# A hybrid encoder layer: the 16 meta keys of attention taken once per head, as rows of one score bank, with one float32r product per group in place of a float32 one

## The chip, the cores and the metric

The kernel runs on one core of one Trainium2 chip. The metric is device time in microseconds (us); of several runs the median counts. A core has a matrix engine (PE; its weight loads are shown apart as PEld), a vector engine (DVE), a scalar engine (ACT), a general engine (POOL), and a queue engine that issues transfers (SP). PE writes into PSUM, which has 8 banks of 128 rows by 512 float32 values; DVE and ACT read and write it.

## The reference

One encoder layer on a sequence of 1024 tokens with 16 learned "meta" tokens ahead of it, 1040 positions in all, model width 1024. All values are float32.

```python
hn = rms_norm(h, ln1_g)
p = hn @ w_in                    # c_q | c_kv | k_rope | x_rnn | x_gate
o_attn = mla_group(...)          # 8 heads; q and k of 96 per head, v of 64
o_rnn = rglru_group(...)         # gated linear recurrence, both directions
h = h + concat(rms_norm(o_attn), rms_norm(o_rnn)) @ w_out
hn = rms_norm(h, ln2_g)
h = h + (silu(hn @ w_gate) * (hn @ w_up)) @ w_down
return h[:, 16:]
```

Within `mla_group`, q and k are normalised per head and rotated, and each query attends to all 1040 keys:

```python
s = einsum('bhqd,bhkd->bhqk', q, k) * 96 ** -0.5
o = einsum('bhqk,bhkd->bhqd', softmax(s), v)
```

The outputs of the meta queries aren't returned and nothing after the attention mixes positions, so the kernel computes attention for the 1024 real queries alone. The meta keys and values are needed.

## The kernel before

**Precision.** PE has a fast product with rounded operands (float32r, F32R in the code) and a slower float32 one. To reach float32 the kernel splits each operand into a rounded part (hi) and the remainder (lo), and adds three float32r products: hi by hi, hi by lo, lo by hi (`mm3`, `hi_lo`, lines 61 to 73). ACT writes hi, DVE subtracts it from the source to give lo.

**Stages by time.** The input projections and the recurrence come first, up to some 197 us. Then come the attention's own projections (`kv_half`, `q_half`, lines 514 to 566), normalisation (`kv_norm`, `q_norm`), and the first head's preparation. The attention loop runs from 257 to 518 us. The output projection and the feed-forward follow up to the end. Most of the program is ordered by a planner; the attention loop (lines 911 to 1000 and on) is under a manual schedule: each engine executes in the order in which the code is written.

**Key blocks.** A head's keys are 8 blocks of 128 real keys (kb 0 to 7) and one block of the 16 meta keys (kb 8), which stand behind the real ones in the tiles `kh`, `kl` (hi and lo of the transposed keys, 96 rows, 1040 columns). The values are in `vhl`: for each real block and head 64 columns of lo, 64 of hi and two columns of ones. The meta values are in `vf` in plain float32: 64 columns and two of ones (line 470, written at line 526).

**The loop.** A group is one head and one half (512) of the queries, so there are 16 groups (`g`, even for the first half, odd for the second) of 9 items each, one item for each key block. One step of the loop handles one item and issues, in this order:

- whatever the step before left in `late` (evacuations, transposes of the next head's q and k, small sums);
- `score`: three products of 512 columns into a bank T (lines 706 to 708), with the keys as weights, and ACT's exponential in place (line 714). A row of ones in the keys and a row with the negated maximum in the queries subtract the maximum. For the meta block the bank has 16 rows only, and the exponential goes to an SBUF tile `e` (lines 709 to 712);
- `max_chunk`: products of the next group's queries with 348 keys each into a bank S, whose maximum DVE reduces (lines 622, 623). There are 12 for a group, spread over the steps by `chunks` (lines 837 to 847);
- `weigh` for the item of two steps before (`LAG` is 2): the values as weights, the exponentials as moving operand, into two banks, A (hi by hi and lo of v by hi, line 743) and B (hi of v by the lo part, line 744), each used by one group at a time. For the meta block it is one float32 product of 16 rows into B (line 748). In the last item the running sums `ah`, `al` go into B too (lines 750, 751);
- `split`: ACT's rounded copy `ph` (line 720), DVE's remainder `pl` (line 721), both in buffers that rotate through `LAG + 2`, and the running sum of `ph` for blocks 0 to 6, on POOL (lines 726, 728). `split_acc` splits that sum: `ah` on ACT, `al` on POOL (lines 734, 735), issued two steps ahead of their use.

At the end of a group ACT and DVE take A and B out (`finish_a`, `finish_b`, lines 753 to 766). `head_prep` (lines 588 to 601) transposes a next head's block and splits it with `hi_lo`; the one for the 16 meta keys is item 2 of an even group. The row of maxima goes to row 96 of the query tile through a DMA on SP (lines 640 to 642). Broadcast reciprocals come by DMA into `bc` (lines 796 to 798), and squares for the next norm into `sqa` (lines 823 to 825).

PSUM in this stage: three banks T, three banks S, one A and one B.

## Time and profile before

| | us |
|---|---|
| median of 3 runs | 1254.62 |
| runs | 1253.25 to 1254.94 |
| the profiled execution's own time | 1253.91 |
| its span, first to last instruction | 1252.1 |
| PE busy | 1227.4 |
| DVE busy | 1007.2 |
| ACT busy | 752.9 |
| POOL busy | 620.4 |
| PEld busy | 993.9 |

In the profile, "busy" is the time in which at least one instruction of that engine runs; matmuls overlap each other, so their durations add up to more, and the distance from one start to the next is what a matmul costs. A group line gives line number, engine, operation, output and input tiles, shapes and count, then busy time and mean ns of one, then the idle time before them and what ended it. A line of waits names the waiting engine, tile and line, what it waited for, the total in us, the number of times, and the longest. A window line gives the length of a stretch, then the busy time of each engine with its count of instructions, then PE's granted clock (1.00 is full), the DMA engines' share, and GB/s. A timeline line gives start and duration in us.

### The profile page before, as it was taken

The page shows a single profiled execution, that of the slowest core. Times are in us where ns is not written, and L with a number is a line of the kernel's source. Part 1 is how long each engine was busy: PE and PEld are TensorE (multiplying, and loading weights), DVE is VectorE, ACT ScalarE, POOL GpSimd, SP SyncE. Part 2 cuts the span into 40 slices and gives each one's busy share as a digit, 9 for nine tenths or more (in the row PEclk, how much of TensorE's full clock was granted, in tenths as well). Part 3 has the DMA queues.
Part 4 walks back from the last instruction along what each step waited for, and adds up shares of the span by engine and source line. Part 5 has one row for each costly group of instructions (what it writes and reads, how often), then busy time and mean ns, then how long its engine had stood idle before and what let it go on. Part 6 is the DMA issues. An engine that isn't in the chain of part 4 may idle for free.

```text
span 1252.1 us, 16541 instructions
## 1 busy us (share of the span) xinstructions
PE 1227.4 (98%) x5698; PEld 993.9 (79%) x5698; DVE 1007.2 (80%) x1579; ACT 752.9 (60%) x1328; POOL 620.4 (50%) x484
## 2 busy tenths in 40 slices
PE   9999999999999999999999999999999999999998
PEld 8899888766666666788788888888888887878887
DVE  8577676899898888699898777777778769987674
ACT  6357775778888877644544433434333345677874
POOL 3401324967788877522543333333333326985564
PEclk9999999999999999999999999999999999999999
DMA  6111011000000020311213223222222137050011
GB/s 237 43 34 43 26 53 48 1 1 2 19 1 18 18 69 1 135 51 34 68 51 102 84 85 102 69 66 89 96 85 84 51 144 327 1 202 1 1 68 68
DMA packets 22797, 83.74 MB, mean 67 GB/s; under 512 B 2836, under 2 KB 4792, under 8 KB 19000
## 3 DMA queue, kind: packets, MB, share of 16 engines
q1 hardware_dynamic: 22712, 82.68, 19.3%
q8 instruction: 45, 0.74, 0.3%
q14 instruction: 40, 0.33, 0.1%
HBM read 68.95 MB, written 13.66 MB: 66 GB/s over the span
## 4 chain that ended last, share of the span: by engine, by line
PE 72%; DVE 4%; ACT 2%; issue 1%; POOL 1%; ACTq 0%; POOLq 0%; DVEq 0%
PE S L72 8%; PE S L73 8%; PE S L71 8%; PE T L72 7%; PE T L71 7%; PE T L73 7%; PE T L706 3%; PE T L708 2%; PE T L707 2%; PE S L622 2%; PE B L744 2%; PE A L743 2%; PE A L71 2%; PE A L73 2%; PE A L72 2%; PE B L73 2%
## 5 line engine op out<-in xcount | busy, mean ns | idle before, releaser
L1189 POOL TENSOR_TENSOR cu<-raw 128x512 f32<-128x512 f32 x109 | 143.7, 1320 | 245.5 <-DVE whl L68 245.5
L67 ACT CAST whl<-cu 128x512 fp32r<-128x512 f32 x120 | 74.2, 622 | 140.2 <-PE T L72 69.8
L1189 POOL TENSOR_TENSOR cu<-big 128x512 f32<-128x512 f32 x68 | 91.9, 1374 | 49.1 <-DVE cu L1226 19.7
L728 POOL TENSOR_TENSOR acc<-acc,ph 128x512 f32<-128x512 f32 x79 | 103.5, 1309 | 13.1 <-ACT ph L720 8.3
L68 DVE TENSOR_TENSOR whl<-cu,whl 128x512 fp32r<-128x512 f32 x120 | 94.3, 787 | 18.5 <-ACT whl L67 18.2
L721 DVE TENSOR_TENSOR pl<-T,ph 128x512 fp32r<-128x512 f32 x128 | 87.7, 685 | 16.9 <-ACT ph L720 16.0
L623 DVE TENSOR_REDUCE mxc<-S 128x1 f32<-128x348 f32 x180 | 87.0, 506 | 2.9 <-PE S L622 2.6
L714 ACT ACTIVATE T<-T 128x512 f32<-128x512 f32 x128 | 74.5, 582 | 23.6 <-PE T L708 18.9
L720 ACT CAST ph<-T 128x512 fp32r<-128x512 f32 x128 | 75.0, 586 | 6.6
L71 PE MATMUL bank<-xh,wh 128*128 128x512 f32 (+3 forms) x208 | 74.7, 359 | 0.6 <-DVE xr L342 0.6
L73 PE MATMUL bank<-xh,wl 128*128 128x512 f32 (+3 forms) x208 | 74.5, 358 | 0.0
L72 PE MATMUL bank<-xl,wh 128*128 128x512 f32 (+3 forms) x208 | 74.4, 358 | 0.0
L67 ACT CAST whl<-raw 128x512 fp32r<-128x512 f32 x44 | 27.4, 623 | 68.7 <-PE S L72 26.6
L706 PE MATMUL T<-ql,kh 96*128 96x512 f32 x144 | 64.2, 446 | 0.8 <-ACT qh L636 0.8
L622 PE MATMUL S<-kh,qh 96*128 96x348 f32 x180 | 53.5, 334 | 4.3 <-DVE mxc L623 3.3
L708 PE MATMUL T<-qh,kh 97*128 97x512 f32 x144 | 57.4, 399 | 0.0
L707 PE MATMUL T<-qh,kl 96*128 96x512 f32 x144 | 57.1, 397 | 0.0
L1189 POOL TENSOR_TENSOR cg<-big 128x512 f32<-128x512 f32 x32 | 42.6, 1343 | 22.5 <-DVE whl L1182 14.5
L744 PE MATMUL B<-pl,vhl 128*66 128x512 f32 x128 | 51.2, 400 | 0.3 <-ACT u L761 0.2
L743 PE MATMUL A<-ph,vhl 128*128 128x512 f32 x128 | 51.2, 400 | 0.0
L622 PEld LDWEIGHTS S<-kh,qh 96*128 96x128 f32 x180 | 33.9, 190 | 19.5 <-DVE mxc L623 5.1
L1138 POOL TENSOR_TENSOR small<-small,sqh 128x512 f32<-128x512 f32 x14 | 19.4, 1384 | 56.3 <-ACT sqh L1137 52.5
(697 smaller groups left out, 4127.6 us busy)
## 6 DMA issues: line engine op xcount, KB each, us to landing
raw<-w_g SPq DMA_DIRECT2D x22, 512.0 KB
raw<-w_u SPq DMA_DIRECT2D x22, 512.0 KB
big<-w_d SPq DMA_DIRECT2D x11, 1024.0 KB
hd<-cu SPq DMA_DIRECT2D x9, 1024.0 KB
big<-hd SPq DMA_DIRECT2D x9, 1024.0 KB
wr<-w_o SPq DMA_DIRECT2D x8, 512.0 KB
hT<-xT SPq DMA_DIRECT2D x8, 512.0 KB
yT<-hT SPq DMA_DIRECT2D x16, 256.0 KB
```

The lines of the kernel that those rows point to most:

```text
L67: act.copy(hi, src)
L68: dve.tensor_sub(lo, src, F(hi))
L71: pe.matmul(ps, wh, xh, start=start, stop=False)
L72: pe.matmul(ps, wh, xl, start=False, stop=False)
L73: pe.matmul(ps, wl, xh, start=False, stop=stop)
L622: pe.matmul(s_[:, :348], qh[:QK, q0 : q0 + P], kh[:QK, k0 : k0 + 348], start=True, stop=True)
L623: dve.reduce_max(mxc[g % 2][:, j, c : c + 1], s_[:, :348], axis=AX.X)
L706: pe.matmul(t, kh[:QK, key(kb)], ql[:QK, q], start=True, stop=False)
L708: pe.matmul(t, kh[:97, key(kb)], qh[:97, q], start=False, stop=True)
L721: dve.tensor_sub(pl, t, F(ph))
L728: eng.tensor_add(o.acc, o.acc, F(ph))
L1189: pool.tensor_tensor(out=t, in0=a, in1=b, op=op)
```

## The change

For a head, the meta keys now get tiles of their own, `kmh` and `kml`, of 160 columns: five blocks of 32, of which the second and the fourth hold the 16 keys twice each and the others are zero. Taken from column 32 on, 128 columns put the scores of the first query half into rows 0 to 31 and 64 to 95 of a bank; taken from column 0 on, those of the second half go into rows 32 to 63 and 96 to 127. Six products (`score_meta`, in the even group's last step) so fill one bank for both halves, each score standing four times, and one exponential of 128 rows covers them. `split_meta` then copies the bank, rounded, into `pm`, and on rows 64 to 127 puts the remainder in place of the copy.

The meta values are split too (`v8`, two more DVE steps for 16 rows), and six DMAs lay them out as `vm`: for each half, hi of v beside the rows of the rounded exponentials, lo of v beside their second copy, hi of v beside the remainders, zero elsewhere. One float32r product of 128 rows for a group then gives all three terms: in the even group's last item, and in the odd group's second item (kb 1). An odd group's last step has no score, no exponential and no split.

`head_prep` for the meta keys makes two products of scale and copy on ACT and two on DVE for `kmh`, `kml`, and a third on ACT for the keys of the maxima, in place of one on each engine. For space, `kl` loses its 16 columns, `mr` has one buffer in place of two, and the square shares the buffer of the broadcast. The maxima of odd groups start one step earlier, with one chunk.

```diff
     vhl = kvp.tile([P, NSP, H, 130], F32R, name="vhl")
-    vf = kvp.tile([P, 1, H, 66], F32, name="vf")
-    pool.memset(vf[:, :, :, 64:66], 1.0)
+    vm = kvp.tile([P, 2, H, 66], F32R, name="vm")
+    pool.memset(F(vm), 0.0)
...
-        t = [pool_.tile([P, n], F32R, name=f"{x}{i}", bufs=1) for x, n in (("qh", S), ("ql", S), ("kh", T), ("kl", T))]
+        t = [pool_.tile([P, n], F32R, name=f"{x}{i}", bufs=1) for x, n in (("qh", S), ("ql", S), ("kh", T), ("kl", S), ("kmh", 160), ("kml", 160))]
         pool.memset(F(t[2][96:97, :]), 1.0)
+        for m in t[4:]:
+            pool.memset(F(m), 0.0)
+        pool.memset(F(meta_blocks(t[4])[96:97]), 1.0)
         return t
+    def meta_blocks(m):
+        return m.rearrange("p (b c) -> p b c", b=5)[:, 1:4:2, :]
...
+    v8 = upp.tile([P, H, 130], F32R, name="v8", bufs=1)
+    pool.memset(F(v8[:, :, 128:130]), 1.0)
...
-            act.activation(vhl[:, b, hs, 64:128] if b < NSP else vf[:n, 0, hs, 0:64], pv[:, :, 64:128], AF.Copy, scale=s)
+            vb = vhl[:n, b] if b < 8 else v8[:n]
+            act.activation(vb[:, hs, 64:128], pv[:, :, 64:128], AF.Copy, scale=s)
...
-            if b < NSP:
-                dve.scalar_tensor_tensor(out=vhl[:n, b, hs, 0:64], in0=pv[:, :, 64:128], scalar=s, in1=F(vhl[:n, b, hs, 64:128]), op0=ALU.mult, op1=ALU.subtract)
+            dve.scalar_tensor_tensor(out=vb[:, hs, 0:64], in0=pv[:, :, 64:128], scalar=s, in1=F(vb[:, hs, 64:128]), op0=ALU.mult, op1=ALU.subtract)
...
             pe.transpose(t[:QK, :NM], src[1][:NM, 4, h, :], ident[:NM, :NM])
+            def meta_out():
+                t2 = t[:QK, :NM].unsqueeze(1).to_broadcast([QK, 2, NM])
+                for b in range(2):
+                    kmh, kml = (meta_blocks(m)[:QK, b].rearrange("p (d c) -> p d c", d=2) for m in dst[4:])
+                    act.activation(kmh, t2, AF.Copy, scale=v(g, 0, QK))
+                    dve.scalar_tensor_tensor(out=kml, in0=t2, scalar=v(g, 0, QK), in1=F(kmh), op0=ALU.mult, op1=ALU.subtract)
+                act.activation(dh[:QK, S : S + NM], t[:QK, :NM], AF.Copy, scale=v(g, 0, QK))
+            return meta_out
...
-            mr = hp0.tile([4, P], F32R, tag="mr", name="mr", bufs=2)
+            mr = hp0.tile([4, P], F32R, tag="mr", name="mr", bufs=1)
...
+    for half in range(2):
+        for r0 in (32 * half, 64 + 32 * half):
+            nc.sync.dma_start(out=F(vm[r0 : r0 + NM, half]), in_=F(v8[:NM, :, 64:130]))
+        nc.sync.dma_start(out=F(vm[32 * half + NM : 32 * half + 32, half, :, 0:64]), in_=F(v8[:NM, :, 0:64]))
...
+    def score_meta(o):
+        qh, ql, _, _, kmh, kml = hset[o.h % 2]
+        t = tbank()
+        for half in range(2):
+            q = slice(512 * half, 512 * half + 512)
+            c = slice(32 - 32 * half, 160 - 32 * half)
+            pe.matmul(t, kmh[:QK, c], ql[:QK, q], start=half == 0, stop=False)
+            pe.matmul(t, kml[:QK, c], qh[:QK, q], start=False, stop=False)
+            pe.matmul(t, kmh[:97, c], qh[:97, q], start=False, stop=half == 1)
+        act.activation(t, t, AF.Exp)
+        return t
+    def split_meta(o, t):
+        o.pm = ap_.tile([P, 512], F32R, tag="ph", name="pm", bufs=LAG + 2)
+        act.copy(o.pm, t)
+        dve.tensor_sub(o.pm[64:128], t[64:128], F(o.pm[64:128]))
...
-        else:
-            pe.matmul(o.B[:66], vf[: nt(kb), 0, o.h, :], o.p[kb], start=False, stop=False)
+        if kb == (1 if o.half else 8):
+            pe.matmul(o.B[:66], vm[:, o.half, o.h, :], groups_[o.g - o.half].pm, start=False, stop=False)
...
-            q = hp1.tile([P, 512], F32, tag="sqa", name="sqa", bufs=1)
+            q = hp1.tile([P, 512], F32, tag="bc", name="sqa", bufs=1)
...
-        i, n = max(0, 9 * (g - 1) - OFF), 0
+        i, n = max(0, 9 * (g - 1) - OFF - g % 2), 0
...
-            t = score(o, kb)
+            if kb < 8:
+                t = score(o, kb)
+            elif o.half == 0:
+                t = score_meta(o)
...
-            if kb < NSP:
+            if kb < 8:
                 split(o, kb, t)
+            elif o.half == 0:
+                split_meta(o, t)
```

More of the change, by code (lines that the diff above doesn't have):

```diff
@@ L615, in max_chunk @@
     def max_chunk(g, i, alloc):
-        qh, _, kh, _ = hset[(g // 2) % 2]
+        qh, _, kh = hset[(g // 2) % 2][:3]
         j, c = divmod(i, 3)
@@ L700, in hymba_layer @@
         pass
+    def score_meta(o):
[13 more added lines that the diff above has]
+        dve.tensor_sub(o.pm[64:128], t[64:128], F(o.pm[64:128]))
     def score(o, kb):
-        qh, ql, kh, kl = hset[o.h % 2]
+        qh, ql, kh, kl = hset[o.h % 2][:4]
         q = slice(512 * o.half, 512 * o.half + 512)
@@ L708, in score @@
         pe.matmul(t, kh[:97, key(kb)], qh[:97, q], start=False, stop=True)
-        if kb >= NSP:
-            e = hp1.tile([P, 512], F32, tag="e", name="e", bufs=1)[: nt(kb)]
-            act.activation(e, t, AF.Exp)
-            o.p.append(e)
-        else:
-            act.activation(t, t, AF.Exp)
+        act.activation(t, t, AF.Exp)
         return t
@@ L746, in weigh @@
                 pe.matmul(o.B[:66], zo, ph, start=False, stop=False)
-        else:
-            pe.matmul(o.B[:66], vf[: nt(kb), 0, o.h, :], o.p[kb], start=False, stop=False)
+        if kb == (1 if o.half else 8):
+            pe.matmul(o.B[:66], vm[:, o.half, o.h, :], groups_[o.g - o.half].pm, start=False, stop=False)
         if kb == 8:
```

## The prediction

> **What bounds the kernel now.** I read the totals first, then the windows of the attention (one row for each head, cut where the meta product starts), then the waits, and last the timelines of single steps.
>
> ```profile
> span 1252.1 us, 16541 instructions
> ```
>
> ```profile
> core 0: us, PE busy (x) PEld busy (x) DVE busy (x) ACT busy (x) POOL busy (x), PEclk, DMA share, GB/s
> 230.00:257.30 27.30, 24.51 (x131) 19.79 (x129) 24.82 (x53) 20.44 (x47) 18.92 (x15) 1.00 0.00 1
> 257.30:290.70 33.40, 32.42 (x154) 23.67 (x154) 30.69 (x60) 26.88 (x49) 26.64 (x21) 1.00 0.01 1
> 290.70:323.04 32.34, 31.39 (x143) 21.45 (x142) 29.05 (x55) 27.13 (x51) 23.67 (x21) 1.00 0.03 9
> 323.04:354.69 31.65, 31.47 (x143) 21.27 (x142) 28.91 (x56) 27.87 (x53) 26.59 (x21) 1.00 0.03 11
> 354.69:386.51 31.82, 31.44 (x144) 21.28 (x143) 29.43 (x56) 27.20 (x51) 26.34 (x22) 1.00 0.02 8
> 386.51:418.05 31.54, 31.31 (x144) 21.16 (x143) 28.41 (x55) 27.67 (x53) 28.48 (x24) 1.00 0.03 11
> 418.05:452.34 34.29, 34.29 (x160) 24.25 (x159) 28.62 (x58) 27.36 (x51) 24.17 (x18) 0.95 0.19 55
> 452.34:483.33 30.99, 30.72 (x140) 20.92 (x139) 27.26 (x53) 27.85 (x52) 25.50 (x20) 1.00 0.09 27
> 483.33:517.51 34.18, 31.51 (x129) 21.01 (x128) 27.73 (x37) 27.08 (x49) 25.29 (x20) 0.95 0.00 1
> 533.00:560.00 27.00, 26.70 (x118) 22.07 (x119) 26.71 (x39) 13.35 (x21) 5.75 (x6) 1.00 0.20 59
> ```
>
> The eight middle rows are the attention, 260.2 us for 8 heads or 16 groups. PE is busy all but 0 to 1.0 us of each row, save the last. VectorE (DVE) comes close behind: in the row from 354.69 it is busy 29.43 of 31.82 us, 92.5%, and only 2.39 us of that head are free. Both must be followed. Who waits for whom in 257 to 518 us:
>
> ```profile
> ACT T L714 <- PE T L708: 18.9, 47, 2.2
> ```
>
> ```profile
> DVE pl L721 <- ACT ph L720: 16.0, 39, 1.0
> ```
>
> ```profile
> PE S L622 <- DVE mxc L623: 3.3, 3, 2.3
> ```
>
> ACT waits for scores from PE, DVE waits for ACT's rounded copy, while PE's own worst wait is 3.3 us in all. So the chain runs from PE to ACT to DVE, and PE sets the pace, with little to spare on DVE. Time taken from PE should show, until DVE's free time is used up.
>
> **The change, part by part. The product.** PE's timeline around one meta product (group 1):
>
> ```profile
> 288.22 0.39 PE L708 MATMUL T<-qh,kh 97*128 97x512 f32 x1
> 288.46 0.32 PE L622 MATMUL S<-kh,qh 96*128 96x348 f32 x1
> 288.61 0.39 PE L743 MATMUL A<-ph,vhl 128*128 128x512 f32 x1
> 288.84 0.39 PE L744 MATMUL B<-pl,vhl 128*66 128x512 f32 x1
> ...
> 290.45 0.32 PE L622 MATMUL S<-kh,qh 96*128 96x348 f32 x1
> 290.70 1.07 PE L748 MATMUL B<-e,vf 16*66 16x512 f32 x2
> 291.70 0.45 PE L750 MATMUL B<-ah,zo 128*66 128x512 f32 x1
> 291.99 0.40 PE L751 MATMUL B<-al,zo 128*66 128x512 f32 x1
> ```
>
> Durations overlap, so costs are read from start to start. A float32r product of 512 columns costs 0.235 us (288.22 to 288.46, 288.61 to 288.84), one of the maxima's chunks 0.15 (288.46 to 288.61). The float32 product runs as two passes: 1.00 to the next start, 0.10 more before it (the chunk ahead takes 0.25 in place of 0.15), 0.05 more behind it (0.29 in place of 0.235). Together 1.15. Its successor is one float32r product at 0.235, so a group gains 0.91 us, a head 1.82, and 16 groups 14.6 us. This is the whole of what can be won.
>
> **The scores.** Six products of 512 columns for a head before, with 16 key columns as weights; six after, with 128 columns. The pitch is set by the 512 moving columns: at L744 (66 columns of weights) and L708 (128) it is the same 0.235 us. So nothing changes in sum. They move: an even group's last step issues six, an odd group's none. The weights now cover 97 rows against zero columns, which has no row of its own; the like loads of L708 run beside the matmuls, and I put it at nothing (if the 0.19 us loads weren't hidden, they would show in L708's pitch now).
>
> **ACT and DVE.** For each head ACT had two exponentials of the 16-row bank; now it has one of 128 rows and one copy.
>
> ```profile
> L720 ACT CAST ph<-T 128x512 fp32r<-128x512 f32 x128 | 75.0, 586 | 6.6
> L714 ACT ACTIVATE T<-T 128x512 f32<-128x512 f32 x128 | 74.5, 582 | 23.6 <-PE T L708 18.9 <-issue 1.1
> ...
> L711 ACT ACTIVATE e<-T 16x512 f32<-16x512 f32 x16 | 9.3, 581 | 2.1 <-PE T L708 2.1
> ```
>
> 581 + 581 ns becomes 582 + 586: no change, plus two small copies of the key at preparation. DVE gets work it didn't have: the subtraction of 64 rows and one more small key operation. Nearest rows:
>
> ```profile
> 323.18 0.68 DVE L757 TENSOR_TENSOR u<-A,u 64x512 f32<-64x512 f32 x1
> 323.78 0.73 DVE L65 SCALAR_TENSOR_TENSOR kl<-S,vec,kh 96x512 fp32r<-96x512 f32 x1
> ...
> 327.75 0.22 DVE L65 SCALAR_TENSOR_TENSOR kl<-S,vec,kh 96x16 fp32r<-96x16 f32 x1
> 327.89 0.51 DVE L623 TENSOR_REDUCE mxc<-S 128x1 f32<-128x348 f32 x1
> ```
>
> 64 x 512 costs 0.60 us start to start, 96 x 16 costs 0.14; with twice the columns, twice, 0.2 more. So 0.8 us a head, 6.4 in all, must fit into DVE's free time: 2.71, 3.29, 2.74, 2.39, 3.13, 5.67, 3.73 and 6.45 us by head (span minus busy). PE's gain shortens a head by 1.82 and DVE needs 0.8 more: the sum, 2.62, is more than the fourth head has and about all that heads 1 and 3 have. DVE thus becomes the second bound in heads 1 to 5. How full can it run? Its highest share in a head is 92.5%; in the last row (533 to 560 us), where it is the bound, 26.71 of 27.00, 99%. With a head's time at (DVE busy + 0.8) / share, and no gain above 1.82, the eight gains sum to 13.6 us at 99%, 2.4 at 92.5%, and 9.4 at 96% (0.6, 1.25, 0.7, 0.35, 1.1, 1.8, 1.8, 1.8). I take 96%, midway: three banks on each side let DVE run ahead a little, but it needs ACT's copy in every step.
>
> **The split sum on POOL.** The last product of a group needs al, which POOL makes from the running sum. In group 5:
>
> ```profile
> 353.88 1.28 POOL L735 TENSOR_TENSOR al<-acc,ah 128x512 fp32r<-128x512 f32 x1
> ```
>
> ```profile
> 355.98 0.40 PE L751 MATMUL B<-al,zo 128*66 128x512 f32 x1
> ```
>
> It is ready at 355.16, 0.82 before its use. And in group 9:
>
> ```profile
> 416.73 1.29 POOL L735 TENSOR_TENSOR al<-acc,ah 128x512 fp32r<-128x512 f32 x1
> ```
>
> ```profile
> 419.33 0.40 PE L751 MATMUL B<-al,zo 128*66 128x512 f32 x1
> ```
>
> There it is 1.31 ahead. In an odd group the last steps lose the float32 product (1.15) and three scores (0.70), so PE comes 1.85 earlier and would wait 1.0 in group 5 and 0.5 in group 9. These are the tightest of the eight odd groups; the others I put at nothing, and the even ones too, where three added scores give most of it back. Against it, ACT has no exponential in that step and rounds the sum up to 0.58 sooner. Of ends 0 and 1.6 I take 1.2.
>
> **Other waits.** The split copy pm takes a turn of the four ph buffers and is last read in the step that refills it, so ACT's copy there waits for one product, up to 0.3 us a head. Behind it stand DVE's subtraction and POOL's sum, both used two steps later; ACT is free 3.8 us in such a head (31.65 - 27.87). Nothing; without that cover 2.4. The square's buffer now is shared with the broadcast one, so two spread DMAs wait for POOL's add; their values are used five steps on. Nothing. The shifted chunks move one of 0.15 us (0.43 on DVE) from an even to an odd group, where a score is missing: nothing in sum.
>
> **The setup.** Six DMAs more on SP, with 18 us until their first use at 275.6; none stands ahead of them there. POOL's memsets:
>
> ```profile
> 197.51 0.75 POOL L512 MEMSET kt<- 128x768 f32 x1
> ...
> 204.22 1.44 POOL L501 TENSOR_TENSOR tabq<-tabs,grope 128x256 f32<-128x256 f32 x2 [1.96 <-DMA grope<-grope]
> ```
>
> 1056 and four times 160 columns at that rate are 1.7 us, of which 1.3 lie before 204.22, in a wait of 1.96. Two DVE steps of the meta values (256 columns, at most 0.60 each) and the small key copies fall in 230 to 257.3, where DVE is busy 24.82 of 27.30 and PE idle for 2.8. Between 0 and 1.4; I take 0.7.
>
> **The sum.** The profiled execution's own time is 1253.91 us (1.8 around its span). 1253.9 - 9.4 + 1.2 + 0.7 = 1246.4. That execution lies 0.7 under the median of the runs shown (1254.62), which is less than the terms' uncertainty, so I give 1246.5.
>
> **The rivals.** *Full gain*: DVE runs as full as at 533 to 560 and al is early: -14.6 + 0.7, 1240.0. For it: PE's waits are few now. Against: five heads would leave DVE next to nothing. *DVE at 92.5%*: its gaps are hand-overs that don't shrink; -2.4 + 1.2 + 0.7, 1253.4, no change that a measurement of this kernel can tell (about 0.2%, 2.5 us). *POOL's al late in every odd group*: half of 9.4 is lost; -4.7 + 0.7, 1249.9. For it: POOL is busy 28.48 of 31.54 in the fifth head; against: only group 5 falls short by more than half a us, by the margins above. *DVE is the pacer and PE merely looks full*: each head keeps its DVE share, so its 0.8 lengthens it by 0.9; 8 x 0.9 + 0.7, 1261.8, slower. It decides once DVE's free time in a head can't be entered by work at all. Against it: DVE's largest wait is for ACT (16.0 us in 39 pieces), and ACT's for PE (18.9 in 47).
>
> The Trainium skill, "Perfetto Trace Analysis", Identifying the Most-Contended Engine, judges TensorE's headroom by the busy share of its weight loads and not of its matmuls, and the vector engine by its occupancy. By that rule DVE with 29.43 of 31.82 us is the most contended here and TensorE with weight loads of 21.28 is not, which is this last rival. The trace speaks against the rule here, since matmuls follow each other at 0.235 us without a gap whatever their weights' size.
>
> **How the numbers follow.** Forecast (gain 3 to 12 us) 0.66; full gain 0.10; al 0.08; DVE at 92.5% 0.08; DVE as pacer 0.08. The range, 1240 to 1253.4, runs from the full gain to DVE at 92.5% and leaves out the slower rival and the outer halves of the two ends. Faster by over 0.2%: the first three less their edge, 0.82; the same: 0.10; slower: 0.08.
>
> **What would show it.** Right: the step from the product before the meta product to the one behind it falls by 0.9 us; heads of 30 to 31 us in place of 31.5 to 32.3 where DVE is fullest; DVE at 95% or more there; PE's waits on DVE's maxima grown by some us; a few waits before L751 in odd groups. Wrong: heads shortened by the full 1.8 with DVE at 97% or more, or heads unchanged with new PE waits of 1.8 us each; a setup longer by more than 1.4 us; or a stage behind 517 us, which no edit touches, that changed its length.

## The result, and the profile after

The changed kernel is slower: 1267.49 us median of 4 runs (1264.41 to 1268.17) against 1253.93 for the kernel before (4 runs, 1252.43 to 1254.94), a ratio on record of 1.0099 with a 95% interval of 1.0085 to 1.0113 (the quotient of the two medians is 1.0108). The forecast was 1246.5, and the range ended at 1253.4. The profiled execution of the changed kernel took 1264.41 us, with a mean granted clock of 0.994. The other three ran at 0.986 to 0.991 and took some 3 us more, so the profile explains 10.5 of the 13.6 us between the medians.

The windows of the changed kernel, cut at the same places as before (the setup first, then the eight heads, then the stretch behind the attention in which DVE is the bound; columns as before):

```profile
core 0: us, PE busy (x) PEld busy (x) DVE busy (x) ACT busy (x) POOL busy (x), PEclk, DMA share, GB/s
240.00:262.83 22.83, 15.71 (x77) 14.19 (x76) 18.10 (x37) 11.71 (x25) 10.62 (x7) 0.85 0.06 9
262.83:295.92 33.09, 31.48 (x150) 23.57 (x151) 29.73 (x61) 25.95 (x49) 25.98 (x23) 1.00 0.01 1
295.92:327.83 31.91, 30.29 (x142) 21.93 (x141) 29.15 (x58) 26.85 (x53) 23.84 (x22) 1.00 0.01 2
327.83:360.34 32.51, 30.87 (x142) 21.56 (x141) 29.57 (x57) 27.51 (x54) 24.80 (x21) 1.00 0.05 17
360.34:393.11 32.77, 30.50 (x142) 21.84 (x141) 29.25 (x57) 27.26 (x54) 26.94 (x23) 1.00 0.01 1
393.11:428.28 35.17, 32.14 (x142) 22.77 (x141) 30.98 (x57) 27.56 (x54) 27.74 (x23) 0.95 0.05 16
428.28:462.57 34.29, 32.49 (x158) 23.53 (x157) 27.50 (x54) 27.19 (x53) 25.42 (x20) 1.00 0.12 36
462.57:495.14 32.57, 30.20 (x139) 21.25 (x138) 28.68 (x57) 28.08 (x54) 24.58 (x20) 1.00 0.15 45
495.14:530.28 35.14, 30.16 (x127) 21.37 (x126) 27.96 (x40) 28.27 (x52) 25.25 (x21) 0.95 0.02 5
...
545.80:572.80 27.00, 26.77 (x118) 22.19 (x119) 26.75 (x39) 13.36 (x21) 5.80 (x6) 1.00 0.21 59
```

The same setup stretch of the kernel before, up to its first score:

```profile
240.00:257.29 17.29, 14.50 (x77) 11.45 (x75) 16.48 (x34) 10.51 (x21) 9.25 (x6) 1.00 0.00 0
```

Two places lost time. The setup (240 us to the first score) ends 5.5 us later (262.84 in place of 257.29), with the same number of matmuls at a granted clock of 0.85 in place of 1.00. And the loop, from the start of the first score to the start of the last product of `ah`, takes 268.4 us in place of 261.2, though its PE work shrank: PE now stands idle for 1.6 to 5.0 us in each head, where it was idle for 0 to 1.0 in all but the last. What lies behind the loop takes 731.3 us after and 733.6 before. So 5.55 + 7.22 - 2.27 = 10.50, the difference of the two profiled executions.

The product itself did what was expected. PE's timeline around the meta product of an odd group:

```profile
382.78 0.39 PE L783 MATMUL B<-pl,vhl 128*66 128x512 f32 x1
383.01 0.40 PE L787 MATMUL B<-pm,vm 128*66 128x512 f32 x1
383.24 0.39 PE L750 MATMUL T<-ql,kh 96*128 96x512 f32 x1
```

It costs 0.23 us from start to start with no gap on either side. The waits of the changed kernel tell what came instead. ACT's waits in 262 to 531 us:

```profile
ACT T L753 <- PE T L752: 19.7, 37, 2.7
ACT kmh L617 <- DVE kml L618: 6.3, 7, 1.6
...
ACT kh L619 <- DVE kml L618: 2.2, 7, 0.3
```

And PE's, in 180 to 530 us:

```profile
PE S L658 <- DVE m L648: 5.9, 7, 1.8
PE B L783 <- ACT u L800: 3.9, 6, 1.0
PE bank L643 <- ACT kh L619: 3.2, 1, 3.2
...
PE B L790 <- POOL al L774: 0.6, 1, 0.6
```

The second and third of ACT's rows have no counterpart before: once per head, seven times in the loop, ACT stands still for 8.5 us in all while it waits for DVE in the preparation of the meta keys. This is `meta_out`, which the change writes as ACT, DVE, ACT, DVE, ACT: copy to `kmh`, remainder to `kml`, the second copy, the second remainder, and the keys of the maxima last. No two of these steps need each other but a copy and its remainder; yet ACT's second copy starts only when DVE's first remainder has ended. All five read one PSUM bank, and the program has an order on them. The Trainium skill, "PSUM — Partial Sum Buffer", PSUM bank collisions raise a hardware error, says that two engines must not access the same bank and rows at once, reads against reads included, and that the compiler adds a dependency between such instructions. The trace agrees as far as it goes: the five steps run strictly one after the other, in the order in which they are written. The third copy is the clean case: it writes `kh`, which neither remainder touches, and still waits for the second one (2.2 us in 7 heads). The second copy could have another reason to wait, since it writes other columns of the same tile that the first remainder reads; no run tells the two reasons apart.

ACT's and DVE's timeline of the changed kernel at that place in one head:

```profile
366.54 0.67 DVE L760 TENSOR_TENSOR pl<-T,ph 128x512 fp32r<-128x512 f32 x1
367.14 0.23 DVE L618 SCALAR_TENSOR_TENSOR kml<-S,vec,kmh 96x32 fp32r<-96x32 f32 x1
367.41 0.28 ACT L617 ACTIVATE kmh<-S,vec 96x32 fp32r<-96x32 f32 x1 [1.63 <-DVE kml L618]
...
368.00 0.27 ACT L619 ACTIVATE kh<-S,vec 96x16 fp32r<-96x16 f32 x1 [0.31 <-DVE kml L618]
368.18 0.58 ACT L753 ACTIVATE T<-T 128x512 f32<-128x512 f32 x1
...
369.41 0.69 DVE L760 TENSOR_TENSOR pl<-T,ph 128x512 fp32r<-128x512 f32 x1 [1.01 <-ACT ph L759]
```

DVE's remainder for the keys (0.23 us) stands in its queue behind a `pl` of 0.67. ACT waits 1.63 us for it, then 0.31 for the second, and the exponential that stands behind them on ACT starts at 368.18; DVE in turn waits 1.01 for the rounded copy that follows. Steps of 0.25 us hold ACT up for 2 us here, since the first remainder has to take its turn behind `pl` in DVE's queue.

In the setup the same five steps lie between larger work, so the last one comes very late, and a maxima product waits for it. ACT, DVE and PE of the changed kernel there:

```profile
245.87 0.23 DVE L618 SCALAR_TENSOR_TENSOR kml<-bank,vec,kmh 96x32 fp32r<-96x32 f32 x1
...
246.13 0.28 ACT L617 ACTIVATE kmh<-bank,vec 96x32 fp32r<-96x32 f32 x1 [0.15 <-DVE kml L618]
...
248.79 0.23 DVE L618 SCALAR_TENSOR_TENSOR kml<-bank,vec,kmh 96x32 fp32r<-96x32 f32 x1
...
249.05 0.27 ACT L619 ACTIVATE kh<-bank,vec 96x16 fp32r<-96x16 f32 x1
...
249.38 0.95 PE L643 MATMUL bank<-kh,qh 96*128 96x348 f32 x2 [3.23 <-ACT kh L619]
250.13 0.52 PE L71 MATMUL bank<-wh,cqh 128*128 128x384 f32 x1
250.45 0.52 PE L72 MATMUL bank<-wl,cqh 128*128 128x384 f32 x1
...
255.79 0.33 PE L71 MATMUL bank<-wh,cqh 128*128 128x384 f32 x1
255.96 0.34 PE L72 MATMUL bank<-wl,cqh 128*128 128x384 f32 x1
```

PE waits 3.23 us for the copy at L619, the last of the five. Then its products of 384 columns follow each other at 0.32 us (250.13 to 250.45) where they took 0.17 before the wait and take 0.17 again at 255.79: for some 5 us PE runs at about half its pace, which is the clock of 0.85 in the window's row. The 12 products of 384 columns in that stretch alone lose 12 x 0.15, 1.8 us, so the wait is paid for a second time in part. The Trainium skill, "TensorE: Matmul & The Clock Gate", What's actually happening, has the clock halved after about 3.4 us without work and full again after as long under load; the trace agrees in kind, with 3.2 us of waiting and some 5 us until the old pace.

### The profile page after: what moved, and what is told of

Same layout as the page of the kernel before. It is cut to its first block, busy times and chain, and to the rows that moved or that the text cites. A ratio compares the mean times of both kernels' runs of the same rounds, so it can differ in the third digit from the quotient of the medians.

```text
span 1262.6 us, 16573 instructions
## 1 busy us (share of the span) xinstructions
PE 1220.0 (97%) x5682; PEld 997.6 (79%) x5682; DVE 1012.1 (80%) x1597; ACT 753.9 (60%) x1344; POOL 621.0 (49%) x491
## 4 chain that ended last, share of the span: by engine, by line
PE 74%; DVE 11%; ACT 7%; issue 4%; POOL 2%; DMA 1%; SPq 0%; ACTq 0%; DVEq 0%; POOLq 0%
PE S L72 8%; PE S L73 8%; PE S L71 8%; PE T L72 7%; PE T L71 7%; PE T L73 7%; PE bank L71 3%; PE bank L72 3%; PE bank L73 3%; DVE pl L760 2%; PE A L72 2%; PE A L73 2%; PE A L71 2%; PE B L73 2%; PE B L72 1%
## 5 line engine op out<-in xcount | busy, mean ns | idle before, releaser
L750 PE MATMUL T<-ql,kh 96*128 96x512 f32 x128 | 57.0, 445 | 1.2 <-DVE ql L65 1.2
L752 PE MATMUL T<-qh,kh 97*128 97x512 f32 x128 | 51.4, 402 | 0.0
L751 PE MATMUL T<-qh,kl 96*128 96x512 f32 x128 | 51.0, 399 | 0.0
```

## The experiments

Theories. *Hand-over*: the loss is the order of the five steps, in the setup and in the loop. *Row*: the chunks of maxima, started a step earlier in odd groups, make the row of maxima late (the 5.9 us of the PE row above). *DVE load*: the added DVE work (subtraction, second remainder) is what the loop can't take. *Cover*: the groups' ends, with fewer products behind which to hide, wait for the evacuation of B (the 3.9 us). Times are medians, ratios are to the kernel before in the same session with a 95% interval, and "loop" is first score to last product of `ah` in the profile, which is one execution. Differences between kernels are given by medians; where the kernels ran in two sessions, the ratios make them up to 1.5 us smaller, and differences of 1 to 2 us are not told from noise.

**Keys first.** The copy for the maxima is the first of the five in place of the last; nothing else moves.

```diff
                 t2 = t[:QK, :NM].unsqueeze(1).to_broadcast([QK, 2, NM])
+                act.activation(dh[:QK, S : S + NM], t[:QK, :NM], AF.Copy, scale=v(g, 0, QK))
                 for b in range(2):
...
-                act.activation(dh[:QK, S : S + NM], t[:QK, :NM], AF.Copy, scale=v(g, 0, QK))
```

> The changed kernel with the copy of the meta keys for the maxima as the first of the five small steps of the meta preparation in place of the last. Theory O: the setup is 5.5 us longer because a chunk of the first maxima waits 3.2 us for this copy, which stands behind two copies and two subtractions; then the loop starts 3 to 4.5 us earlier than 262.8 and the time falls by as much, about 1263 to 1264. Theory D: the setup is longer because of DVE's added work there (two value steps and two key steps, 1.3 us); then the chunk's wait moves to DVE and the loop's start gains 1 us or less.

1256.03 us, ratio 1.0019 (1.0004 to 1.0033): 11.5 us of the changed kernel's median are gone (10.0 by the ratios), more than the 5.5 of the setup and than the 3 to 4.5 that were expected. The setup ends at 259.21 with a clock of 1.00; the loop is 262.9, another 5.5 less. There the wait between `kmh` and `kml` is still present (5.5 us, 7 times), while ACT's third step no longer stands between DVE's second remainder and the next exponential; that this is the whole of the 5.5 is only argued.

**All of ACT's copies first, then DVE's two remainders.** The same five instructions and values, with one hand-over in place of four.

```diff
-                for b in range(2):
-                    kmh, kml = (meta_blocks(m)[:QK, b].rearrange("p (d c) -> p d c", d=2) for m in dst[4:])
+                ms = [[meta_blocks(m)[:QK, b].rearrange("p (d c) -> p d c", d=2) for m in dst[4:]] for b in range(2)]
+                act.activation(dh[:QK, S : S + NM], t[:QK, :NM], AF.Copy, scale=v(g, 0, QK))
+                for kmh, _ in ms:
                     act.activation(kmh, t2, AF.Copy, scale=v(g, 0, QK))
+                for kmh, kml in ms:
                     dve.scalar_tensor_tensor(out=kml, in0=t2, scalar=v(g, 0, QK), in1=F(kmh), op0=ALU.mult, op1=ALU.subtract)
-                act.activation(dh[:QK, S : S + NM], t[:QK, :NM], AF.Copy, scale=v(g, 0, QK))
```

> The changed kernel with the meta preparation in another order: the keys for the maxima first, then ACT's two other copies, and only then DVE's two subtractions. In the changed kernel ACT's second copy waits for DVE's first subtraction and its third for the second (a semaphore stands there in the program, since both engines read the same PSUM bank), 6.3 + 2.2 us of ACT in seven heads. Theory H (hand-over): ACT loses that time and PE after it; then the loop is 6 to 9 us shorter than the changed one's 268.4, the setup 3.5 shorter, and the total 1251 to 1255, under the kernel with the keys first (1256.0). Theory D (load): DVE's added work sets the time whatever ACT waits for; then the loop stays at the 262.9 of the kernel with the keys first, total 1255 to 1257.

1253.04 us, ratio 0.9992 (0.9982 to 1.0002), loop 259.0. Undoing the order alone takes 14.4 us off the changed kernel (13.4 by the ratios), 3.0 more than the keys first alone, and ACT no longer waits for `kml` at all. The kernel is then level with the one before, not faster. PE's largest waits in it, in 230 to 531 us:

```profile
PE B L784 <- ACT u L801: 3.5, 6, 1.0
PE bank L609 <- DVE vhl L542: 2.9, 1, 2.9
```

The first is the wait for B's evacuation, the second a wait in the setup for DVE's value step, behind which the granted clock from 240 us to the first score is 0.91; the wait for the row of maxima has shrunk from 5.9 us to 1.3.

**The same order put into the kernel before.** The reverse: its two steps for the meta keys are written twice and a third copy is added, all with the values that it had, so that ACT and DVE alternate as in the changed kernel. The float32 product and everything else stay.

```diff
+        def out():
+            hi_lo(dh[:QK, c], dl[:QK, c], t[:QK, :w], v(g, 0, QK))
+            if half == 2:
+                hi_lo(dh[:QK, c], dl[:QK, c], t[:QK, :w], v(g, 0, QK))
+                act.activation(dh[:QK, c], t[:QK, :w], AF.Copy, scale=v(g, 0, QK))
+        return out
```

> The kernel before with its preparation of the 16 meta keys written out as ACT copy, DVE subtraction, ACT copy, DVE subtraction, ACT copy (the same values written again): three small steps of 0.27 and 0.14 to 0.2 us more for each head, and ACT waiting twice for DVE. Theory H: the waits are the cost, not the work; 8 to 12 us slower than before, with the setup's part, 1262 to 1266. Theory D: only the work counts, 0.6 us of ACT and 0.15 of DVE in 8 heads hidden in their free time; under 2 us.

1266.13 us, ratio 1.0099 (1.0084 to 1.0114): 11.75 us slower, the same ratio as the whole change. ACT's waits in it (230 to 531 us):

```profile
ACT kh L64 <- DVE kl L65: 6.5, 7, 1.5
...
ACT kh L606 <- DVE kl L65: 2.1, 7, 0.3
```

These are the rows of the changed kernel, 6.3 and 2.2, within 0.2 us; PE waits 3.9 us for the last copy in the setup, and the clock from 240 us to its first score is 0.84. Its loop is 268.0 us, about the changed kernel's 268.4, although PE still has the float32 products. That the order costs this much is shown from both sides. What the bank alone contributes is not: here the repeated copy also overwrites the columns that the remainder ahead of it reads.

**The shift of the chunks undone**, in the changed kernel.

```diff
-        i, n = max(0, 9 * (g - 1) - OFF - g % 2), 0
+        i, n = max(0, 9 * (g - 1) - OFF), 0
```

> The changed kernel with the maxima of odd groups back at their old step (the g % 2 of the chunks' start left out). Theory O (order): the row of maxima is transposed on PE one step earlier in even groups, right behind the next head's preparation on DVE, and waits there for DVE (7.0 us of new time between the B product and the row's transposes, 8 groups); then this kernel is 5 to 7 us faster than the changed one, about 1260 to 1262. Theory D (load): DVE and ACT are short of time whatever the order, and the wait only moves to the next place; then it gains under 2 us, 1265 or more.

1263.37 us, ratio 1.0067 (1.0050 to 1.0084), loop 267.6, 0.8 less than with the shift. The median is 4.1 lower, but the two traces differ by 1.3 only; the other runs of the changed kernel had a lower clock (0.986 to 0.991) than these (0.992 to 0.996). The 5.9 us wait for the row is gone, and this one stands in its place on PE:

```profile
PE S L643 <- DVE ql L65: 4.2, 6, 1.5
```

So the loop's loss stays when the row's wait goes, and another PE instruction waits instead. The row theory falls as the cause of the loop's 7.2 us. Whether the shift costs the changed kernel 3 us in its runs at a lower clock stays open.

**The row of maxima one step later in odd groups**, in the changed kernel.

```diff
-        rows_[i] = g
+        rows_[i + g % 2] = g
```

> The changed kernel with its shifted chunks kept, but the row of maxima of odd groups reduced and transposed one step later, at the step of the kernel before. If only the early transposes hurt (theory O), it gains the same 5 to 7 us as the kernel without the shift. If the shift of the chunks is itself bad or good, the two differ by over 1 us. Theory D: under 2 us.

1264.10 us, ratio 1.0072 (1.0057 to 1.0087), loop 268.5: nothing in the loop, and a median 3.4 lower, the same finding.

**The shift undone with ACT first**: the kernel with ACT's copies first, and the edit of the shift above.

```diff
-        i, n = max(0, 9 * (g - 1) - OFF - g % 2), 0
+        i, n = max(0, 9 * (g - 1) - OFF), 0
```

> The kernel with ACT's copies first, and the maxima of odd groups back at their old step as well. The shift taken back from the changed kernel took 0.8 us off its loop. Theory H: the same again, within 1.5 us of the kernel with ACT's copies first. Were the early row of maxima a cost of its own, it would be 3 us or more faster than that.

1253.20 us, ratio 0.9986 (0.9977 to 0.9995). Against 1253.04, with ACT's copies first, the shift is worth nothing either way.

**Without DVE's subtraction**, ACT first. Rows 64 to 127 of `pm` keep the rounded copy, so the kernel leaves out the remainder's term and adds the rounded one twice.

```diff
         act.copy(o.pm, t)
-        dve.tensor_sub(o.pm[64:128], t[64:128], F(o.pm[64:128]))
```

> The kernel with ACT's copies first and without DVE's subtraction on rows 64 to 127 of the meta bank (0.60 us a head; the remainder of the meta exponentials is left out). Theory D: DVE sets the pace, and 8 times 0.6, so 3 to 5 us, is gained. Theory H: DVE has room in that step, where the odd group's last step has no split; 0 to 1.5 us.

1254.35 us, ratio 0.9997 (0.9988 to 1.0006). Taking 0.6 us a head from DVE gains nothing.

**What the product alone is worth.** The kernel before with one float32r product of the 16 rows and no other edit. It leaves out the meta block's remainders, of the exponentials and of the values.

```diff
-    vf = kvp.tile([P, 1, H, 66], F32, name="vf")
+    vf = kvp.tile([P, 1, H, 66], F32R, name="vf")
...
-            e = hp1.tile([P, 512], F32, tag="e", name="e", bufs=1)[: nt(kb)]
+            e = hp1.tile([P, 512], F32R, tag="e", name="e", bufs=1)[: nt(kb)]
```

> The kernel before with the meta exponentials and the meta values merely rounded to float32r, so that the meta product is one pass; the remainders of both are left out, and nothing else is changed. It takes the PE gain alone, without new work on DVE or ACT and without a new order. Theory that PE paces the loop: 0.91 us for each of 16 groups, 12 to 14.6 us faster than before, 1239 to 1242. Theory that DVE and ACT pace it already: 0 to 5 us faster. Between these: PE's lead is caught by DVE's and ACT's bursts in part, 6 to 11.

1248.10 us, ratio 0.9944 (0.9929 to 0.9958), loop 254.2. PE's timeline shows why 14.6 us could not be had here:

```profile
290.87 0.32 PE L622 MATMUL S<-kh,qh 96*128 96x348 f32 x1
291.11 0.44 PE L748 MATMUL B<-e,vf 16*66 16x512 f32 x1
291.49 0.44 PE L750 MATMUL B<-ah,zo 128*66 128x512 f32 x1
291.77 0.39 PE L751 MATMUL B<-al,zo 128*66 128x512 f32 x1
```

A product of 16 rows between products of 128 takes 0.38 to the next start, some 0.09 more ahead of it (0.24 in place of 0.15) and 0.045 behind (0.28 in place of 0.235): 0.52 in place of 0.235. So 1.15 falls by 0.63, and 16 groups gain 10 at most.

**The same, padded to 128 rows.** Exponentials and values stand in tiles of 128 rows, zero below row 15. What is left out is the same as in the last kernel.

```diff
-    pool.memset(F(vf[:, :, :, 64:66]), 1.0)
+    pool.memset(F(vf), 0.0)
+    pool.memset(F(vf[:NM, :, :, 64:66]), 1.0)
...
+    e = hp1.tile([P, 512], F32R, name="e", bufs=1)
+    pool.memset(F(e), 0.0)
...
-            act.activation(e, t, AF.Exp)
+            act.activation(e[:NM], t, AF.Exp)
...
-            pe.matmul(o.B[:66], vf[: nt(kb), 0, o.h, :], o.p[kb], start=False, stop=False)
+            pe.matmul(o.B[:66], vf[:, 0, o.h, :], o.p[kb], start=False, stop=False)
```

> The kernel before with the one-pass meta product (remainders of the meta block left out), its weights and exponentials padded with zero rows from 16 to 128. In the one-pass kernel with 16 rows the product took 0.37 us to the next start, with 0.10 more ahead of it and 0.05 behind it, 0.52 in all, where products of 128 rows take 0.235. If the row count is what costs this, the three gaps go back to 0.235 and 0.15 and up to 4.6 us more are free on PE; the time is 1244 to 1247 if half of it or more shows, 1248 if ACT and DVE eat it. If the gaps stay, the row count isn't the cause.

1245.63 us, ratio 0.9936 (0.9924 to 0.9948), the fastest of all kernels here. The same place on PE:

```profile
290.34 0.32 PE L623 MATMUL S<-kh,qh 96*128 96x348 f32 x1
290.50 0.39 PE L750 MATMUL B<-e,vf 128*66 128x512 f32 x1
290.74 0.40 PE L752 MATMUL B<-ah,zo 128*66 128x512 f32 x1
290.97 0.39 PE L753 MATMUL B<-al,zo 128*66 128x512 f32 x1
```

0.16, 0.24 and 0.23: the full 0.91 us is off PE in each group. The time gains 8.8 of 14.6 (8.0 by the ratio), so a part of PE's gain is lost even with no other edit.

**Where that part goes: DVE or ACT.** First the 16-row kernel with DVE's 64-row subtraction once more in block 7 of each even group, 0.6 us a head:

```diff
         dve.tensor_sub(pl, t, F(ph))
+        if kb == 7 and o.half == 0:
+            dve.tensor_sub(pl[64:128], t[64:128], F(ph[64:128]))
```

> The kernel before with the one-pass product (remainders of the meta block left out, 6.4 us faster than before), and with one subtraction of 64 rows by 512 columns more on DVE for each head (a part of pl of block 7 written twice with the same values), so 0.6 us a head and no other change of order. Theory D: the load alone costs 3 to 5 us, so 1251 to 1253. Theory H: under 1.5 us, 1248 to 1249.6.

1248.20 us, ratio 0.9948 (0.9934 to 0.9961), against 1248.10 without it: 4.8 us of added DVE work cost nothing that these intervals (some 1.7 us to each side) resolve, less than the 3 to 5 us expected of a DVE bound. Then the padded kernel with ACT's rounded copy of block 7 made twice, 0.6 us a group, 9.6 in all:

```diff
         act.copy(ph, t)
+        if kb == 7:
+            act.copy(ph, t)
```

> The padded one-pass kernel (remainders of the meta block left out, 1245.6) with ACT's rounded copy of block 7 made twice (the same values), 0.6 us more of ACT for each group, 9.6 us in all, and no wait on another engine between. Theory L (ACT is the second bound): 4 to 9 us slower, 1250 to 1255. If ACT has room wherever it doesn't wait: under 2 us, below 1247.6.

1250.50 us, ratio 0.9972 (0.9959 to 0.9984), 4.9 above the padded kernel. Its runs differ in granted clock (0.993 to 0.997, the padded kernel's 0.996 and 0.997); the one run at 0.997 took 1249.13, which is 2.8 above the mean of the padded kernel's runs at that clock. So about a third to a half of ACT's added time comes out at the end. ACT, busy for 85% of the padded kernel's loop, then looks closer to the bound than DVE at 91%. That is in part argued: ACT got twice the dose, in a kernel with less PE work, and its second copy stands ahead of block 7's remainder, so that DVE starts later too.

**The small copies in the best order**, three on ACT and two on DVE, added to the padded kernel:

```diff
+            for _ in range(3):
+                act.activation(dh[:QK, c], t[:QK, :w], AF.Copy, scale=v(g, 0, QK))
+            for _ in range(2):
+                dve.scalar_tensor_tensor(out=dl[:QK, c], in0=t[:QK, :w], scalar=v(g, 0, QK), in1=F(dh[:QK, c]), op0=ALU.mult, op1=ALU.subtract)
```

> The padded one-pass kernel with the preparation of the meta keys as three ACT copies and then two DVE subtractions (the same values again), the load that the shared bank's preparation has in its best order, without the shared bank: 0.5 us of ACT and 0.15 of DVE a head. Theory L: part of the 6.6 us between the two loops comes from here, 2 to 4 us slower, 1248 to 1250. If the shared bank's moved scores are what costs: under 1.5 us, below 1247.1.

1247.22 us, ratio 0.9949 (0.9937 to 0.9962): 1.6 us, hardly clear of noise. The same five steps in the alternating order cost 11.75 in the kernel before.

**Cover, first form.** ACT first, with B taken out whole right behind the group's last product:

```diff
             if kb2 == 8:
-                late.append(lambda o2=o2: finish_b(o2))
+                finish_b(o2)
```

> The kernel with ACT's copies first in the meta preparation, and the copy that takes bank B out issued right behind the group's last product, ahead of that step's rounded copy, in place of at the start of the next step. Theory C (cover): the float32 product stood between the scores of that step and the next group's first B product, and its 1.15 us hid ACT's exponential, copy and B copy; without it PE waits between the A and the B product (9 us of excess there in the kernel with ACT's copies first, 1.2 before). Then 3 to 6 us are gained, 1247 to 1250. Rival theory D: ACT is merely full, and the wait goes to the next score or product; under 1.5 us.

1269.37 us, ratio 1.0114 (1.0096 to 1.0131), 16.3 us above the kernel that it edits, and no test of the theory: B's wait went, but the edit moved two transfers on SP past each other. ACT's wait and SP's order in this kernel:

```profile
ACT wh L67 <- DMA wr<-w_o: 10.6, 2, 6.7
```

```profile
437.38 0.60 SPq L804 DMA_DIRECT2D sr<-u  x1
438.02 0.45 SPq L914 DMA_DIRECT2D wr<-w_o  x1
```

The load of `w_o` is issued at 438.02, behind `sr`, which waits for the end of a group; without the edit it was issued at 428.99, ahead of it. The second load fell behind a `sr` too (issued at 462.69). ACT waits 10.6 us for the two in the loop. The padded kernel with the same edit gave the same, with 9.5 us of waiting for `w_o`:

```diff
             if kb2 == 8:
-                late.append(lambda o2=o2: finish_b(o2))
+                finish_b(o2)
```

> The padded one-pass kernel with the copy of bank B issued right behind the last product. Theory C: 1 to 3 us faster than without it, 1242 to 1246. Theory D: the same within 1 us.

1261.13 us, ratio 1.0054 (1.0040 to 1.0067), 15.5 above the padded kernel.

**Cover, second form.** Only ACT's copy of B is made early; the rest of `finish_b`, its transfers too, stays where it was. With ACT first:

```diff
+    def b_copy(o):
+        o.u2 = otp.tile([P, 512], F32, tag="u2", name="u2")
+        act.copy(o.u2[:66], o.B[:66])
...
-        o.u2 = u2 = otp.tile([P, 512], F32, tag="u2", name="u2")
-        act.copy(u2[:66], o.B[:66])
+        u2 = o.u2
...
             if kb2 == 8:
+                b_copy(o2)
                 late.append(lambda o2=o2: finish_b(o2))
```

> The kernel with ACT's copies first in the meta preparation, and only ACT's copy out of bank B moved ahead of that step's rounded copy; the transfer and the add behind it stay in the next step. With the transfer moved too, the time had grown by 16 us, 10.6 of it ACT waiting for a weight transfer that now stood behind that one on SP's queue, while the excess between A and B products fell from 8.9 to 3.3. Theory C (the float32 product covered the copy of B): without the queue's trouble 3 to 6 us faster than 1253.0, so 1247 to 1250. Theory D: ACT is full and the wait only moves; 1252 to 1254.

1254.89 us, ratio 1.0011 (1.0002 to 1.0020). Read from PE's starts, B's wait shrinks from some 8.9 us of gaps between the products into A and B to 3.4, and the gaps ahead of the chunks of maxima grow from some 2.6 to 7.4. The padded kernel with the same edit:

```diff
             if kb2 == 8:
+                b_copy(o2)
                 late.append(lambda o2=o2: finish_b(o2))
```

> The padded one-pass kernel (remainders of the meta block left out; 1245.6) with ACT's copy out of bank B ahead of the rounded copy. Theory C: 1 to 3 us faster, 1242.5 to 1244.5. Theory D: within 1 us.

1250.11 us, ratio 0.9966 (0.9954 to 0.9978), 4.5 slower than without it (3.8 by the ratios). That the copy, put early on ACT, makes the next exponential late is argued. Cover falls as a way to gain.

**A meta bank for each group**, ACT first. Each half has its own bank, exponential and split in its own group, so the scores are no longer six in one step and none in the other.

```diff
-        for half in range(2):
+        for half in (o.half,):
...
-        if kb == (1 if o.half else 8):
-            pe.matmul(o.B[:66], vm[:, o.half, o.h, :], groups_[o.g - o.half].pm, start=False, stop=False)
+        if kb == 8:
+            pe.matmul(o.B[:66], vm[:, o.half, o.h, :], o.pm, start=False, stop=False)
...
-            elif o.half == 0:
+            else:
                 t = score_meta(o)
```

> The kernel with ACT's copies first, but each group with a meta bank of its own: three scores, one exponential of 128 rows, a copy and a subtraction in its last step, and its product two steps later. PE has the same products as with one bank for a head; ACT gets 1.17 us and DVE 0.6 us more per head. Theory B (bunching): the six scores in one step and none in the other cost the 6.6 us by which the loop with one bank for a head is longer than the padded one-pass kernel's; then 1247 to 1251. Theory L (load of ACT and DVE): 1254 to 1260.

1252.63 us, ratio 0.9989 (0.9981 to 0.9998), 0.4 from the kernel that it edits. It undoes the bunching and adds a full exponential, copy and subtraction per head; either the two cancel or neither matters, and this run can't tell which.

## Why the prediction was wrong, step by step

**The failed step** is the sentence "no change, plus two small copies of the key at preparation", with the setup's "small key copies" inside a term of 0.7. The instructions were counted and priced as work, and their work is indeed small (1.6 us in the best order, in the padded kernel). What was not asked is in which order two in-order queues would meet on one bank. The prediction named, for `pm` and the broadcast, what is queued behind a waiting instruction; for these five it named no wait. The runs put 11.75 us on the order when it is added to the kernel before, and 14.4 when it is taken from the changed one: 11.5 by moving one copy to the front, 3.0 by the rest. This isn't the whole miss. With the order mended the kernel takes 1253.04, still 6.5 over the forecast, because the gain of 9.4 did not come either.

**The setup** was given 0.7, at most 1.4. It was 5.5: 3.6 from the keys copy standing last (262.84 against 259.21 with keys first), a wait of 3.2 us and the low clock after it. The other 1.9 is still 0.5 over the upper end that was given, but the first score moves by up to 2 us between kernels whose setups are the same (257.91 and 259.96 in the two padded ones without and with ACT's added copy).

**The gain on PE** was right as work and wrong as time. The step of 0.91 us a group is there (0.23 in place of 1.15). But with nothing else changed it gives 8.8 us, interval 6.5 to 9.5, of 14.6. The prediction did foresee that a second bound takes part of it, and its 9.4 is near that figure. That nearness is luck: 9.4 was worked out for DVE's added 0.8 us a head, which the padded kernel doesn't have, at a DVE share of 96% chosen midway between 2.4 and 13.6.

**DVE as the second bound** failed. In the changed kernel DVE is busy 80 to 91% of a head, not the 95% that was expected where it is fullest, though its work in the eight rows grew by 2.7 us; adding 0.6 a head (the DVE run, in the 16-row kernel) or taking it away (the run without subtraction, ACT first) moves the time by no more than noise. ACT's added time does show. The slower rival, *DVE as pacer*, came out closest in number (1261.8) and speaks of a mechanism that the same two runs exclude; the nearness is luck. The rule named beside it (the Trainium skill, "Perfetto Trace Analysis", Identifying the Most-Contended Engine) fails here too: by occupancy DVE was the engine to watch, and 4.8 us of added work on it cost 0.1.

**al on POOL**: the place was right, group 5 alone, and the wait 0.6 us where 1.0 was worked out; group 9's 0.5 did not come. **The chunks' shift** at nothing in sum was right with ACT's copies first; in the changed kernel its wait of 5.9 us could be removed with 0.8 us or nothing gained in the loop, and the lower medians of those two runs (4.1 and 3.4) are open. **pm's buffer** showed no wait of ACT's. **The broadcast**'s wait came: SP stands 5.9 us in two places (3.4 the longest) for POOL's add, but no engine is seen waiting for the broadcast values, so the price of nothing fits. **B's evacuation** (3.9 us in 6 waits, 0.2 before) was foreseen nowhere; removing it only moved it. **The stage behind 517 us** became 2.3 of 733.6 us shorter, which no edit explains; it is 731.3 to 731.5 in the four kernels with the change's order or keys first, and 732.7 to 732.9 in those with ACT's copies first, so it isn't the chance of one trace.

**What stays open.** With the order mended, the changed kernel does the same work on PE as the padded one and is 7.4 us slower (1253.04 against 1245.63). The small copies are 1.6 of it. The setup is 1.8 in these two traces (259.68 against 257.91, the wait for the value step on DVE is there), and less in others (258.50 with the shift undone). The other 4 are in the loop and not settled: the subtraction, the shift, the early copy of B and the bunching of scores were each undone by itself, and none gave it back. On PE most of it lies between the products into A and B: 128 steps from A's start to the next start take 38.8 us against 34.0. Why 5.8 us of PE's gain do not arrive in the padded kernel is settled only so far that added DVE load did not show and added ACT load did.

## What to carry to other kernels

Steps of two engines on one PSUM bank are a chain in the order in which they are written: write all of one engine's first, and first of all the one for which somebody waits. Price a small step by the queue it stands in, not by its own time, most of all where PE waits at the end, since waits of 2.9 to 3.9 us in the setup here also cost the clock (0.91 to 0.84). Before a second bound is named by its busy share, add half a microsecond of idle work to each candidate, the same dose in the same kernel, and see which moves the time.

## What the runs showed of the hardware that was not expected

**Few rows.** A float32r product with 16 rows of weights among products with 128 costs 0.52 us, and 0.235 when it is padded with zeros to 128 rows (the two timelines above). The whole kernel gained 2.5 us by the padding (1248.10 to 1245.63), or 1.0 by the ratios, whose intervals overlap. The Trainium skill, "TensorE: Matmul & The Clock Gate", Why this matters for your kernels, has a single product of 32 rows take as long as one of 128. No run here has that case; one of 16 rows among full ones costs more, by 0.28 us.

**The clock after a wait.** Stretches at about half the pace follow shorter waits than 3.2 us too, and some follow no wait. PE's timeline of the changed kernel in the fifth head, whose row shows 0.95:

```profile
403.97 0.27 PE L658 MATMUL S<-ident,m 128*4 128x128 f32 x1 [1.80 <-DVE m L648]
...
404.54 0.40 PE L752 MATMUL T<-qh,kh 97*128 97x512 f32 x1
...
405.95 0.63 PE L751 MATMUL T<-qh,kl 96*128 96x512 f32 x1
406.37 0.63 PE L752 MATMUL T<-qh,kh 97*128 97x512 f32 x1
...
409.40 0.39 PE L734 MATMUL T<-ql,kmh 96*128 96x512 f32 x1
```

After a wait of 1.80 us the first products run as usual, then for some 3 us they take 0.42 from start to start in place of 0.235, and from 409.40 on 0.23 again. After a wait of 2.68 us at 506.40 the same came, in the last row at 0.95. But the wait alone doesn't decide it. In the first run with B taken out early, no such stretch follows a wait of 1.81 us that ends at 360.04. And in the kernel before, one stands in the row from 418.05, in which PE is busy all the time (34.29 of 34.29 us):

```profile
449.07 0.63 PE L744 MATMUL B<-pl,vhl 128*66 128x512 f32 x1
449.50 0.63 PE L746 MATMUL B<-ph,zo 128*66 128x512 f32 x1
```

What stands ahead of it there is 1.7 us of products of one column (from 446.02); whether they bring it about isn't tested. Waits of 1.8 and 2.7 us are shorter than the 3.4 us after which the Trainium skill, in the section named with the setup, has the clock fall.

**SP's order.** A load that fell behind another transfer on SP, which waits for the end of a group, was issued 9 us later. With the next load, which fell behind the same way, the kernel took 16.3 us more, the most of any single edit here; ACT waited 10.6 us for the two, and moving the copy of B without the transfers cost 1.9.
